# A decoder layer on one core: the second load of attention branch weights is issued ahead of the reads that spread the softmax reciprocals, and its pieces are split behind the rounding of the heads

## The chip, the core and the metric

The kernel runs on one core of a Trainium2 chip. The core has TensorE for matmuls (PE in the profile, with the weight load before each matmul as PEld), VectorE (DVE), ScalarE (ACT), GpSimd (POOL) and SyncE (SP). SP issues nearly all the transfers of this kernel; they go through one queue that 16 DMA engines serve. The metric is the device time of one execution in microseconds (us), the median of several runs; less is better.

## What is computed

One decoder layer on 256 tokens of width 1024, in float32, with random weights:

```python
h = rmsnorm(x, norm_mix_g)
proj = h @ w_in
q, k, v, u_pool, gate_logits = jnp.split(proj, [...], axis=-1)
q = apply_partial_rotary(rmsnorm(heads(q), q_norm_g), pos)      # 8 heads of 64
k = apply_partial_rotary(rmsnorm(heads(k), k_norm_g), pos)
attn = moba_attention(q, k, heads(v))    # 256 tokens are one block: causal softmax attention
pooled = multiscale_pool_mixer(u_pool, w_pool, pool_scale)
gates = jax.nn.sigmoid(gate_logits + b_gate).reshape(B, S, N_BRANCHES, D)
mixed = gates[:, :, 0] * (attn @ w_branch_attn) + gates[:, :, 1] * (pooled @ w_branch_pool)
x = x + mixed @ w_out
h2 = rmsnorm(x, norm_ffn_g)
up = causal_depthwise_conv(h2 @ w_up, conv_w, conv_b)
gate, val = jnp.split(up, 2, axis=-1)
return x + (jax.nn.silu(gate) * val) @ w_down
```

## The kernel before

**Matmuls in three.** A float32 product is made of three matmuls on rounded operands: each operand is split into a rounded high part (`hi`, written by ScalarE, `high`, L92) and the rest (`lo`, written by VectorE, `low`, L96), and `mm3` (L104 to L106) multiplies high by high, rest by high and high by rest. Every weight is therefore loaded raw, then split by ScalarE and VectorE, and only then used by TensorE.

**Weights as a list.** `order` lists all weight chunks of 1 MB in the order of use: q, k, v, pooling input (p), gates (g), pooling map, the pooling branch (`bp`, two chunks), the attention branch (`ba`, two chunks), the output projection (`o`, four) and the FFN. Four raw buffers exist (`RAWBUFS`), so chunk c can be loaded once chunk c-4 has been split. `load` issues the next one on SP, `loads` issues as many as have a free buffer. Each chunk is split in two pieces of 128 x 1024. `next_high` puts the high part of the next piece on ScalarE, unless its chunk is four or more ahead of the oldest one in use; `next_low` puts the rest on VectorE, one piece behind the high part, or at once with `eager=True`. `ahead()` does one of each.

**Engines run in program order.** Each engine works its instructions in the order in which they are written, so an instruction that waits holds up all behind it on that engine; the order is written out by hand. `later(n, fn)` puts a step off until `tick()` has been called n more times; `tick()` runs once for each of the 16 gate tiles and then at every odd j of the loop that follows.

**Attention to branches.** The softmax numerators (weights) of the last two head pairs are turned by VectorE, spilled to memory (`spill`), and read back transposed by `fill_weights` (SP, eight reads into `sm`). The sums' reciprocals go the same way: `turn_weights` spills them (`home_sums`, L297), and `fill_late` (L615) reads them back, spread over 64 partitions at a time, as `RS` (L623, two reads of 256 KB). `fill_late` also lets a weight load go ahead of these reads, and then takes off the brake on loads (`paused`).

**The loop of the pooling branch** (L738 to L753) runs over j = 0 to 7. Step j makes one tile `ps_bp` on TensorE (12 matmuls) in one of four PSUM banks, so step j needs the bank that step j-4 has given back. VectorE gives a bank back by multiplying the tile into its gate (L751, at j = 4 and 5 L741), and applies the norm's factor to one plain gate (L753). At j = 4 (`VALUES`) TensorE also makes `ps_o`, the attention values (L635, 32 matmuls), and `rounded` multiplies them by `RS` on VectorE (L654, four) and writes the high part of `heads` on ScalarE (four). At j = 5 `rests` writes the rest of `heads` on VectorE (four). In between, each j calls `ahead()` once.

**The loop of the attention branch** comes behind it: eight tiles `ps_ba` (L104 to L106) from `heads` and the `ba` chunks, in the same four banks. VectorE multiplies each into its gate (L766), GpSimd adds the other branch (L767), ScalarE and VectorE write `mh` and `ml`, and the output projection `ps_out` reads these.

Of the kernel before, what the change touches and what calls it, by code (L numbers as in the profile page):

```python
# [55 lines left out]
MAPS = 6  # L56
VALUES = 4
LATE = 9
GATES = (4, 5, 0, 1, 2, 6, 7, 3)
PLAIN = (4, 5, 6, 7, 8, 9)  # L60
HALVED = 2
# [10 lines left out]
def hybrid_layer_kernel(ctx: ExitStack, tc: tile.TileContext, xq_d, xtok_d, par_d, wkv_d, wpg_d,  # L72
# [21 lines left out]
    def low(lo, hi, src, scale=None):  # L94
        if scale is None:
            nc.vector.tensor_tensor(lo, src, hi.bitcast(F32), ALU.subtract)  # L96
        else:
            nc.vector.scalar_tensor_tensor(lo, src, scale, hi.bitcast(F32), ALU.mult, ALU.subtract)
# [11 lines left out]
    order += [("v", wkv_d[2 + c]) for c in range(2)] + [("p", wpg_d[c]) for c in range(2)]  # L110
    order += [("g", wpg_d[2 + c]) for c in GATES[:MAPS]] + [("pool", wpool_d)]
    order += [("g", wpg_d[2 + c]) for c in GATES[MAPS:]]
    order += [("bp", wbp_d[c]) for c in range(2)] + [("ba", wba_d[c]) for c in range(2)]
# [10 lines left out]
    def load(parts=1):  # L124
        c = loaded[0]
        if c == len(order):
            return
        loaded[0] += 1
        name, src = order[c]
        n = src.shape[-1]  # L130
        if c in cut_loads:
            parts = 2
        raws[c] = raw_p.tile([P, CH], F32, tag="raw", name=f"raw_{name}{c}")
        for i in range(parts):
            sl = slice(i * n // parts, (i + 1) * n // parts)
            nc.sync.dma_start(out=raws[c][:, sl], in_=src[:, sl])

    def raw(c, sl):

        if order[c][0] != "q":  # L140
            return raws[c][:, sl]
        at = sl.start % 512
        return xq[:, 4 * c + sl.start // 512, S + at:S + at + sl.stop - sl.start]
# [21 lines left out]
    def next_high():  # L165
        if at[0] < len(pieces):
            c, sl, first, _ = pieces[at[0]]
            if c - oldest() >= WBUFS:
                return
            at[0] += 1  # L170
            if first:
                moving = order[c][0] in "qkv"
                place = MOVING if moving else 0
                his[c] = whi_p.tile([P, CH + P], F32R, tag="whi", name=f"hi_{order[c][0]}{c}")[:, place:]
                place = MOVING if moving else FAR
                los[c] = wlo_p.tile([P, CH + P], F32R, tag="wlo", name=f"lo_{order[c][0]}{c}")[:, place:]
            high(his[c][:, sl], raw(c, sl))

    def next_low(eager=False):
        if at[1] < at[0] - STAGGER or at[0] == len(pieces) > at[1] or (at[1] < at[0] and eager):  # L180
            c, sl, _, last = pieces[at[1]]
            at[1] += 1
            low(los[c][:, sl], his[c][:, sl], raw(c, sl))
            if last:
                split.add(c)
                loads()
# [3 lines left out]
    def loads(most=None):  # L190

        while loaded[0] - RAWBUFS in split and order[loaded[0] - RAWBUFS][0] != "q" and loaded[0] < len(order):
            if paused[0] if most is None else most == 0:
                break
            load()
            most = most if most is None else most - 1
# [3 lines left out]
    def ahead(upto=0):  # L200

        next_high()
        next_low()
        if at[1] - sum(p[0] < used[0] for p in pieces) < upto:
            next_high()
            next_low()

    def chunk(name):
        c = used[0]
        used[0] += 1  # L210
        spent.update(i for i in range(c) if order[i][0] != "dn")
        assert order[c][0] == name and all(p[0] != c or name == "dn" and p[3] for p in pieces[at[1]:]), (name, order[c][0])
        return his[c], los[c]
# [130 lines left out]
    def big(name):  # L344
        return tmp.tile([P, 2 * 2 * 3 * P], F32, tag="big", bufs=2, name=name)
# [87 lines left out]
    def later(n, fn, *args):  # L433
        due.setdefault(clock[0] + n, []).append((fn, args))

    def tick():
        clock[0] += 1
        for fn, args in due.pop(clock[0], []):
            fn(*args)
# [80 lines left out]
    def gate(n):  # L520
        return gates[:, n // 2, n % 2, :]
# [27 lines left out]
    def scores():  # L549
        for hp in (0, 2, 3, 1):  # L550
            pss[hp] = score_steps(hp)

    def masked(hps):
        if hps[0] == 0:
            ys, sms = big("y0"), big("sm0")
        else:
            sms, ys = (act.tile([P, 2 * 2 * 3 * P], F32, tag=tag, name=f"{name}2")
                       for tag, name in (("qk", "sm"), ("at", "y")))
        for i, hp in enumerate(hps):
            ps = pss[hp]  # L560
            on = slice(i * 6 * P, (i + 1) * 6 * P)
            sm = sms[:, on].rearrange("p (j c) -> p j c", j=2)
            mx = tmp.tile([P, 2, 2], F32, tag="mx", name=f"mx{hp}")
            for j in range(2):
                nc.vector.tensor_tensor(sm[:, j, TOK[0]], ps[j][:, 3 * P:4 * P], mask[:, 1, :], ALU.add)
            for j in range(2):
                for t in (1, 0):
                    nc.vector.tensor_tensor_reduce(sm[:, j, TOK[t]], ps[j][:, TOK[t]],
                                                   whole if t else sm[:, j, TOK[0]], 1.0, LOWEST,
                                                   ALU.add, ALU.max, mx[:, t, j:j + 1])  # L570
            nc.vector.scalar_tensor_tensor(mx, mx, -1.0, qs[:, :, 2 * hp:2 * hp + 2], ALU.mult, ALU.mult)
            if i == 0:
                exponentials(hp, sm, mx, ys[:, on], sms[:, on])
            else:
                behind.append((exponentials, hp, sm, mx, ys[:, on], sms[:, on]))
# [35 lines left out]
    def fill_weights(hp, home, sm):  # L611
        fill(home, sm)
        soft[hp] = sm.rearrange("p (a n r) -> p a n r", a=4, r=32)

    def fill_late(far):  # L615

        for weights in late:
            fill_weights(*weights)
        loads(1)
        RS.append(big("RS"))  # L620
        for j in range(2):
            src = far.rearrange("(a i) r -> a (i r)", a=4)[None, :, j * S:(j + 1) * S].to_broadcast([DH, 4, S])
            nc.sync.dma_start(out=RS[0][j * DH:(j + 1) * DH, 0:H // 2 * S].rearrange("p (a c) -> p a c", a=4), in_=src)  # L623
        paused[0] = False
        loads()
# [22 lines left out]
    def rounded(hps, po):  # L648
        if not heads:
            both = act.tile([P, 2, KA, S], F32R, tag="at", name="heads")  # L650
            heads.extend(both[:, i] for i in range(2))
        for i, hp in enumerate(hps):
            v = weighed(hp)
            nc.vector.tensor_tensor(v, po[:, i, 0:S].rearrange("p (a t r) -> p a t r", a=4, r=32), v, ALU.mult)  # L654
            high(tokens(heads[0], hp), natural(hp))
# [31 lines left out]
    for n in range(2 * KD):  # L687
# [7 lines left out]
        if n == 6:  # L695
            scores()
        if n in (6, LATE):
            masked((0, 1) if n == 6 else (2, 3))
        if n == LATE - 1:
            paused[0] = True  # L700
# [12 lines left out]
        held.clear()  # L713
        f = 2 * GATES[b] + c
        if n in PLAIN:
# [10 lines left out]
    def branch(src, oph, opl, j, w):  # L726
        hi, lo = w
        ps = bank(f"ps_b{src}{j}")
        for k in range(4):
            sl = slice(k * 512 + (j % 4) * P, k * 512 + (j % 4 + 1) * P)  # L730
            mm3(ps[:, 0:S], (hi[:, sl], lo[:, sl]), (oph[:, k, :], opl[:, k, :]), k == 0, k == 3)
        return ps

    for j in range(KD):
        if j % 4 == 0:
            w = chunk("bp")
        ps = branch("p", poolh, pooll, j, w)
        if j == VALUES:  # L738
            pos = [(hps, values(hps)) for hps in ((0, 1), (2, 3))]
        if j in (VALUES, VALUES + 1):  # L740
            nc.vector.tensor_tensor(gate(KD + j), ps[:, 0:S], gate(KD + j), ALU.mult)  # L741
            for hps, po in pos:
                rounded(hps, po) if j == VALUES else rests(hps)
        if j % 2 == 1:
            tick()
            ahead()
        if j in (0, 2, 4, 6):
            ahead()
        sigmoids(1)
        if j not in (VALUES, VALUES + 1):  # L750
            nc.vector.tensor_tensor(gate(KD + j), ps[:, 0:S], gate(KD + j), ALU.mult)  # L751
        if j < len(plain):
            nc.vector.tensor_tensor(gate(plain[j]), gate(plain[j]), R1, ALU.mult)  # L753
# [264 lines left out]
```

## Time and profile before

| what | us |
|---|---|
| median of 3 runs | 333.08 (331.98 to 333.25) |
| the profiled execution, its own time | 332.71 |
| its span in the profile | 330.9 |
| TensorE matmul busy | 324.2 |
| VectorE busy | 259.3 |
| ScalarE busy | 202.0 |
| GpSimd busy | 71.4 |

How to read it: the span runs from the first to the last instruction, and the profiled execution's own time is 1.8 us longer. A matmul is pipelined: its row says 276 ns, but the next one starts 0.11 us after it, so TensorE is "busy" without a break as long as matmuls follow each other. Rows of a timeline give start, duration, engine, line, operation, output and inputs; "[0.53 <-DVE xq L751]" at a row's end says that the engine was idle for 0.53 us before it and that VectorE's instruction on L751 ended that. Names that end in q (SPq) are an engine's sequencer, here the issue of a transfer; the landing of a transfer is in the view of DMA issues.

### The profile page before, as it was taken

The page shows a single profiled execution, that of the slowest core. Times are in us where ns is not written, and L with a number is a line of the kernel's source. Part 1 is how long each engine was busy: PE and PEld are TensorE (multiplying, and loading weights), DVE is VectorE, ACT ScalarE, POOL GpSimd, SP SyncE. Part 2 cuts the span into 40 slices and gives each one's busy share as a digit, 9 for nine tenths or more (in the row PEclk, how much of TensorE's full clock was granted, in tenths as well). Part 3 has the DMA queues.
Part 4 walks back from the last instruction along what each step waited for, and adds up shares of the span by engine and source line. Part 5 has one row for each costly group of instructions (what it writes and reads, how often), then busy time and mean ns, then how long its engine had stood idle before and what let it go on. Part 6 is the DMA issues. An engine that isn't in the chain of part 4 may idle for free.

```text
span 330.9 us, 6770 instructions
## 1 busy us (share of the span) xinstructions
PE 324.2 (98%) x2708; PEld 316.8 (96%) x2708; DVE 259.3 (78%) x451; ACT 202.0 (61%) x329; POOL 71.4 (22%) x89
## 2 busy tenths in 40 slices
PE   8999999999999799999999999999999999999996
PEld 8888899999998699999999999999999999999995
DVE  4939989989974976878997977777777776768844
ACT  5767618566955756768676766564646464646520
POOL 1007690000000043130331212121212121221330
PEclk9999999999999999999999999999999999999999
DMA  7999799737699741763629274545455555553003
GB/s 265 425 415 215 241 367 292 277 131 280 229 267 361 261 186 18 254 240 128 210 64 360 104 282 146 237 150 236 169 213 165 218 184 198 193 189 129 0 2 127
DMA packets 16542, 69.72 MB, mean 211 GB/s; under 512 B 2176, under 2 KB 7040, under 8 KB 9856
## 3 DMA queue, kind: packets, MB, share of 16 engines
q1 hardware_dynamic: 16096, 69.17, 59.6%
q8 instruction: 21, 0.34, 0.4%
q10 hardware_dynamic: 416, 0.13, 0.3%
q14 instruction: 9, 0.07, 0.1%
HBM read 65.61 MB, written 3.69 MB: 209 GB/s over the span
## 4 chain that ended last, share of the span: by engine, by line
PE 80%; DVE 10%; DMA 5%; POOL 1%; issue 1%; ACT 1%; SPq 0%; DVEq 0%; POOLq 0%
PE ps_up L105 12%; PE ps_up L104 12%; PE ps_up L106 12%; PE ps_d L879 6%; PE ps_d L878 6%; PE ps_d L880 6%; PE ps_q L334 4%; DMA raw_o<-in_wout 3%; PE ps_k L334 3%; PE ps_v L334 3%; PE ps_out L105 2%; PE ps_out L106 2%; PE ps_out L104 2%; DMA raw_bp<-in_wbp 2%; PE ps_g L104 2%; PE ps_g L106 2%
## 5 line engine op out<-in xcount | busy, mean ns | idle before, releaser
L106 PE MATMUL ps_up<-hhi,lo_up 128*128 128x256 f32 x352 | 97.2, 276 | 0.0
L104 PE MATMUL ps_up<-hhi,hi_up 128*128 128x256 f32 x352 | 97.2, 276 | 0.0
L105 PE MATMUL ps_up<-hlo,hi_up 128*128 128x256 f32 x352 | 97.2, 276 | 0.0
L105 PEld LDWEIGHTS ps_up<-hlo,hi_up 128*128 128x128 f32 x352 | 66.1, 188 | 0.0
L104 PEld LDWEIGHTS ps_up<-hhi,hi_up 128*128 128x128 f32 x352 | 66.1, 188 | 0.0
L106 PEld LDWEIGHTS ps_up<-hhi,lo_up 128*128 128x128 f32 x352 | 66.1, 188 | 0.0
L96 DVE TENSOR_TENSOR lo_up<-raw_up,hi_up 128x1024 fp32r<-128x1024 f32 x44 | 54.7, 1261 | 7.3 <-ACT hi_up L92 7.3
L880 PE MATMUL ps_d<-ah,lo_dn 128*128 128x256 f32 x176 | 48.6, 276 | 0.0
L878 PE MATMUL ps_d<-ah,hi_dn 128*128 128x256 f32 x176 | 48.6, 276 | 0.0
L879 PE MATMUL ps_d<-al,hi_dn 128*128 128x256 f32 x176 | 48.6, 276 | 0.0
L92 ACT ACTIVATE hi_up<-raw_up 128x1024 fp32r<-128x1024 f32 x44 | 44.1, 1046 | 0.0
L860 POOL TENSOR_TENSOR c_v<-c_g,c_v 128x256 f32<-128x256 f32 x22 | 16.2, 738 | 121.4 <-DVE c_v L843 121.4
L92 ACT ACTIVATE ah<-c_v 128x256 fp32r<-128x256 f32 x22 | 9.2, 418 | 45.6 <-POOL c_v L860 45.6
L104 PE MATMUL ps_g<-xhi,hi_g 128*128 128x256 f32 x128 | 35.4, 277 | 0.0
L106 PE MATMUL ps_g<-xhi,lo_g 128*128 128x256 f32 x128 | 35.3, 276 | 0.0
L105 PE MATMUL ps_g<-xlo,hi_g 128*128 128x256 f32 x128 | 35.3, 276 | 0.0
L879 PEld LDWEIGHTS ps_d<-al,hi_dn 128*128 128x128 f32 x176 | 33.0, 188 | 0.0
L878 PEld LDWEIGHTS ps_d<-ah,hi_dn 128*128 128x128 f32 x176 | 33.0, 188 | 0.0
L880 PEld LDWEIGHTS ps_d<-ah,lo_dn 128*128 128x128 f32 x176 | 33.0, 188 | 0.0
L96 DVE TENSOR_TENSOR lo_dn<-raw_dn,hi_dn 128x1024 fp32r<-128x1024 f32 x22 | 27.8, 1264 | 0.4 <-ACT hi_dn L92 0.4
L848 DVE TENSOR_TENSOR u_v<-ps_up,R 128x256 f32<-128x256 f32 x22 | 9.3, 421 | 20.9 <-PE ps_up L106 20.8
L885 POOL TENSOR_TENSOR al<-c_v,ah 128x256 fp32r<-128x256 f32 x22 | 22.0, 1002 | 11.6 <-ACT ah L92 11.6
(189 smaller groups left out, 781.5 us busy)
## 6 DMA issues: line engine op xcount, KB each, us to landing
raw_up<-in_wup SPq DMA_DIRECT2D x22, 1024.0 KB, 4.8
raw_g<-in_wpg SPq DMA_DIRECT2D x8, 1024.0 KB, 7.4
raw_dn<-in_wdn SPq DMA_DIRECT2D x8, 1024.0 KB, 4.9
raw_o<-in_wout SPq DMA_DIRECT2D x4, 1024.0 KB, 11.1
raw_dn<-in_wdn SPq DMA_DIRECT2D x6, 512.0 KB, 4.9
raw_v<-in_wkv SPq DMA_DIRECT2D x2, 1024.0 KB, 15.5
raw_p<-in_wpg SPq DMA_DIRECT2D x2, 1024.0 KB, 13.0
raw_bp<-in_wbp SPq DMA_DIRECT2D x2, 1024.0 KB, 5.6
```

The costliest lines, as they stand in the source:

```text
L92: nc.scalar.activation(hi, src, AF.Copy, scale=scale)
L96: nc.vector.tensor_tensor(lo, src, hi.bitcast(F32), ALU.subtract)
L104: nc.tensor.matmul(out, sh, mh, start=start, stop=False, **kw)
L105: nc.tensor.matmul(out, sh, ml, start=False, stop=False, **kw)
L106: nc.tensor.matmul(out, sl, mh, start=False, stop=stop, **kw)
L334: nc.tensor.matmul(pt[t][:, c:c + wide], sx[:, k, t * P:(t + 1) * P], wx[:, sl], start=k == 0 and c == 0 and sx is xhi and wx is hi, stop= ...
L848: nc.vector.tensor_tensor(u, ps[:, 0:S], R2, ALU.mult)
L860: nc.gpsimd.tensor_tensor(uc[1], g[1], uc[1], ALU.mult)
L878: nc.tensor.matmul(o, hi[:, sl], acch[i], start=first, stop=False, skip_group_check=True)
L879: nc.tensor.matmul(o, hi[:, sl], accl[i], start=False, stop=False, skip_group_check=True)
L880: nc.tensor.matmul(o, lo[:, sl], acch[i], start=False, stop=i == KF - 1, skip_group_check=True)
L885: nc.gpsimd.tensor_tensor(accl[i], act_i, acch[i].bitcast(F32), ALU.subtract)
```

## The change

```diff
+PIECES = (1, 1, 0, 0, 0, 2, 1, 1)
 ...
 def fill_late(far):
     for weights in late:
         fill_weights(*weights)
+    loads(1)
+    later(1, spread, far)
+
+def spread(far):
+
     loads(1)
     RS.append(big("RS"))
     for j in range(2):
 ...
         if j % 2 == 1:
             tick()
+        for _ in range(PIECES[j]):
             ahead()
-        if j in (0, 2, 4, 6):
-            ahead()
+        if j == 2:
+            next_low(eager=True)
         sigmoids(1)
```

`fill_late` issues one weight load (ba0, the first chunk of the attention branch) and puts the reads of `RS` off by a tick into `spread`, which issues one more load (ba1, the second chunk) ahead of them. In the loop of the pooling branch, `ahead()` is no longer called once for each j, but 1, 1, 0, 0, 0, 2, 1 and 1 times; at j = 2 the rest of the third piece is written at once. The lines behind the change stand 1 to 7 lower in the new file (L751 is L758, L654 is L660).

On SP the place is the end of the reads of the attention weights (`sm`). Before:

```order
L305 DMA sm_1007<-home_w_1102 32x4x192 x4
L136 DMA raw_ba_1145<-in_wba 128x2048
L623 DMA RS<-home_sums 64x4x256 x2
L136 DMA raw_ba_1170<-in_wba 128x2048
L136 DMA raw_o_1237<-in_wout 128x2048
```

Now:

```order
L306 DMA sm_1007<-home_w_1102 32x4x192 x4
L137 DMA raw_ba_1145<-in_wba 128x2048
L137 DMA raw_ba_1192<-in_wba 128x2048
L629 DMA RS<-home_sums 64x4x256 x2
L137 DMA raw_o_1237<-in_wout 128x2048
```

The second load of `ba` has changed places with the two reads of `RS`; nothing else moved on SP.

On VectorE the place is j = 4 to 7 of the loop of the pooling branch, from the multiplication by `RS` on; `lo_ba` is the rest of the last piece of ba1, `lo_o` that of the first piece of the output weights, and xq holds the gates. Before:

```order
L654 TENSOR_TENSOR RS<-ps_o_1393,RS 128x4x64 x2
L654 TENSOR_TENSOR RS<-ps_o_1402,RS 128x4x64 x2
L96 TENSOR_TENSOR lo_ba_1338<-raw_ba_1170,hi_ba_1337 128x1024
L753 TENSOR_TENSOR xq<-xq,R_169 128x256
L741 TENSOR_TENSOR xq<-ps_bp_1429,xq 128x256
L96 TENSOR_TENSOR heads<-RS,heads 128x256 x4
L96 TENSOR_TENSOR lo_o_1422<-raw_o_1237,hi_o_1421 128x1024
L753 TENSOR_TENSOR xq<-xq,R_169 128x256
L751 TENSOR_TENSOR xq<-ps_bp_1451,xq 128x256
```

Now:

```order
L660 TENSOR_TENSOR RS<-ps_o_1392,RS 128x4x64 x2
L660 TENSOR_TENSOR RS<-ps_o_1401,RS 128x4x64 x2
L760 TENSOR_TENSOR xq<-xq,R_169 128x256
L747 TENSOR_TENSOR xq<-ps_bp_1422,xq 128x256
L97 TENSOR_TENSOR heads<-RS,heads 128x256 x4
L97 TENSOR_TENSOR lo_ba_1338<-raw_ba_1192,hi_ba_1337 128x1024
L760 TENSOR_TENSOR xq<-xq,R_169 128x256
L97 TENSOR_TENSOR lo_o_1442<-raw_o_1237,hi_o_1441 128x1024
L758 TENSOR_TENSOR xq<-ps_bp_1449,xq 128x256
```

The rest of ba1's last piece went from ahead of the rests of `heads` to behind them, and `lo_o` went behind the next multiplication of a gate (L753).

On ScalarE the place is the same stretch, from the high part of ba1's first piece on; xq<-xq,par are the sigmoids of the gates. Before:

```order
L92 ACTIVATE hi_ba_1337<-raw_ba_1170 128x1024
L666 ACTIVATE xq<-xq,par 128x256
L92 ACTIVATE hi_ba_1337<-raw_ba_1170 128x1024
L666 ACTIVATE xq<-xq,par 128x256 x2
L92 ACTIVATE heads<-RS 128x256 x4
L92 ACTIVATE hi_o_1421<-raw_o_1237 128x1024
```

Now:

```order
L93 ACTIVATE hi_ba_1337<-raw_ba_1192 128x1024
L672 ACTIVATE xq<-xq,par 128x256 x3
L93 ACTIVATE heads<-RS 128x256 x4
L672 ACTIVATE xq<-xq,par 128x256
L93 ACTIVATE hi_ba_1337<-raw_ba_1192 128x1024
L93 ACTIVATE hi_o_1441<-raw_o_1237 128x1024
```

The high part of ba1's last piece went from ahead of the high parts of `heads` to behind them. TensorE's and GpSimd's rows are the same as before.

## The prediction

> **What bounds the kernel now.** The page first. TensorE is busy for nearly the whole span and heads the chain that ended last; only VectorE and transfers take a visible share of that chain besides.
>
> ```profile
> PE 324.2 (98%) x2708; PEld 316.8 (96%) x2708; DVE 259.3 (78%) x451; ACT 202.0 (61%) x329; POOL 71.4 (22%) x89
> PE 80%; DVE 10%; DMA 5%; POOL 1%; issue 1%; ACT 1%; SPq 0%; DVEq 0%; POOLq 0%
> ```
>
> So a change can gain only where TensorE waits. The view of waits, for PE alone, names these waits, and but for the start there are two, both in the stretch that the change touches:
>
> ```profile
> PE ps_ba L105 <- DVE heads L96: 1.7, 1, 1.7
> PE ps_bp L104 <- DVE xq L751: 0.5, 1, 0.5
> ```
>
> TensorE's timeline shows their places, and a third place where single matmuls stand apart:
>
> ```profile
> 106.15 0.82 PE L635 MATMUL ps_o<-sm,vn 128*64 128x256 f32 x8
> ...
> 108.27 0.28 PE L106 MATMUL ps_bp<-poolh,lo_bp 128*128 128x256 f32 x1
> 109.07 0.39 PE L104 MATMUL ps_bp<-poolh,hi_bp 128*128 128x256 f32 x1 [0.53 <-DVE xq L751]
> ...
> 111.91 0.28 PE L104 MATMUL ps_ba<-heads,hi_ba 128*128 128x256 f32 x1
> 113.86 0.38 PE L105 MATMUL ps_ba<-heads,hi_ba 128*128 128x256 f32 x1 [1.67 <-DVE heads L96]
> ...
> 126.53 0.28 PE L106 MATMUL ps_out<-mh,lo_o 128*128 128x256 f32 x1
> 126.72 0.38 PE L104 MATMUL ps_out<-mh,hi_o 128*128 128x256 f32 x1
> 127.25 0.39 PE L105 MATMUL ps_out<-ml,hi_o 128*128 128x256 f32 x1
> 127.47 0.28 PE L106 MATMUL ps_out<-mh,lo_o 128*128 128x256 f32 x1
> ```
>
> Without a wait the next matmul starts 0.11 us after the last. By that pace j = 6 (109.07) starts 0.69 late, the second matmul of `ps_ba` (113.86) 1.84 late, each with one slow restart (0.11 more), and the output projection loses 0.08, 0.42 and 0.11 at 126.72, 127.25 and 127.47. Together some 3.4 us: about what there is to win.
>
> What ends these waits is VectorE, and what held VectorE is seen on its own timeline and ScalarE's:
>
> ```profile
> 99.30 1.06 ACT L92 ACTIVATE hi_ba<-raw_ba 128x1024 fp32r<-128x1024 f32 x1 [1.05 <-DMA raw_ba<-in_wba]
> 102.41 0.50 ACT L666 ACTIVATE xq<-xq,par 128x256 f32<-128x256 f32 x1
> 106.36 1.06 ACT L92 ACTIVATE hi_ba<-raw_ba 128x1024 fp32r<-128x1024 f32 x1 [3.46 <-DMA raw_ba<-in_wba]
> ```
>
> ```profile
> 101.53 0.41 DVE L751 TENSOR_TENSOR xq<-ps_bp,xq 128x256 f32<-128x256 f32 x1
> 104.01 0.41 DVE L753 TENSOR_TENSOR xq<-xq,R 128x256 f32<-128x256 f32 x1
> 107.45 1.22 DVE L96 TENSOR_TENSOR lo_ba<-raw_ba,hi_ba 128x1024 fp32r<-128x1024 f32 x1 [3.03 <-ACT hi_ba L92]
> 108.60 0.42 DVE L751 TENSOR_TENSOR xq<-ps_bp,xq 128x256 f32<-128x256 f32 x1
> ...
> 110.27 1.40 DVE L654 TENSOR_TENSOR RS<-ps_o,RS 128x256 f32<-128x256 f32 x4
> 111.59 1.21 DVE L96 TENSOR_TENSOR lo_ba<-raw_ba,hi_ba 128x1024 fp32r<-128x1024 f32 x1
> ...
> 113.39 1.42 DVE L96 TENSOR_TENSOR heads<-RS,heads 128x256 fp32r<-128x256 f32 x4
> ...
> 116.87 0.41 DVE L766 TENSOR_TENSOR xq<-ps_ba,xq 128x256 f32<-128x256 f32 x1
> ```
>
> ScalarE waited 3.46 us for ba1 to land, VectorE 3.03 for ScalarE. From 107.45 to 116.87, 9.42 us, no VectorE row has a bracket: it works off a backlog. Bank 2 comes back late (L751 at 108.60, TensorE's first wait), the rests of `heads` come late (the second), and the first tile of the attention branch is taken only at 116.87. **The bound is the landing of ba1.** It is set by its place in the queue. The issues and landings, from SP's timeline and the view of DMA issues over windows that hold one issue each (last figure: us to landing):
>
> ```profile
> 93.95 0.43 SPq L136 DMA_DIRECT2D raw_ba<-in_wba  x1
> raw_ba<-in_wba SPq DMA_DIRECT2D x1, 1024.0 KB, 5.2
> 94.43 0.68 SPq L623 DMA_DIRECT2D RS<-home_sums  x1
> 95.15 0.66 SPq L623 DMA_DIRECT2D RS<-home_sums  x1
> RS<-home_sums SPq DMA_DIRECT2D x1, 256.0 KB, 7.4
> 95.90 0.56 SPq L136 DMA_DIRECT2D raw_ba<-in_wba  x1
> raw_ba<-in_wba SPq DMA_DIRECT2D x1, 1024.0 KB, 10.4
> 96.57 0.36 SPq L136 DMA_DIRECT2D raw_o<-in_wout  x1
> raw_o<-in_wout SPq DMA_DIRECT2D x1, 1024.0 KB, 12.2
> 97.42 0.33 SPq L136 DMA_DIRECT2D raw_o<-in_wout  x1
> raw_o<-in_wout SPq DMA_DIRECT2D x1, 1024.0 KB, 13.8
> ```
>
> They land in order of issue: ba0 at 93.95 + 5.2 = 99.15, the second read of `RS` at 102.55, ba1 at 106.3, the first two output chunks at 108.8 and 111.2. A megabyte with nothing small ahead of it follows 2.4 to 2.5 us behind the last; ba1 needed 7.15 behind ba0, so the reads of `RS`, half a megabyte, delayed it by 4.7.
>
> **The change, part by part.** It adds and removes no instruction; four moves are to be priced.
>
> *ba1 ahead of `RS`.* It takes the issue slot at 94.43, and lands one megabyte behind ba0, at 99.15 + 2.45 = 101.6. ScalarE's queue reaches its first piece behind the sigmoid of 102.41, which takes 0.40 with one more behind it, so at 102.81; the high part is ready at 103.87. VectorE is free at 104.01 + 0.34 = 104.35. So `lo_ba`, at 107.45 before, starts at 104.35: **3.10 us earlier**, with 1.6 us of slack for the landing (the high part must be ready by 104.35). Bank 2 is back at about 105.9, and TensorE asks for it at 108.39: the first wait goes whole.
>
> *`RS` behind ba1.* The same bytes in another order are through at 106.3, so `RS` lands by then (at 105.0, if its reads take the 3.4 us that they took behind ba0). VectorE wants it 2.82 us after `lo_ba` (107.45 to 110.27), at 107.17; the values are ready at 106.15 + 0.82 = 106.97. Cost nothing; cover 0.9 us, and each us beyond that costs one.
>
> *The last piece of ba1 behind the heads' rounding.* On VectorE 1.13 us leave the path to the rests of `heads`: these start at 107.17 + 4 x 0.33 + 0.33 (L753) + 0.33 (L741) = 109.16, where L741 finds its tile done at 108.27 + 0.28. TensorE reaches the second matmul of `ps_ba` 24 matmuls and one behind 108.39, at 111.2, and the rests are written at 0.33 us each from 109.6 on: the second wait goes whole, 1.6 us to spare. The piece itself is then run at 110.5 and needed only by the attention branch's fifth tile. Its high part stands on ScalarE behind the rounding (done at about 109.0) and a sigmoid, and is ready at 110.4, just in time. What is queued behind: L753, `lo_o`, and L751 for j = 6, which gives TensorE the bank of its third `ps_ba` tile. By the same durations that ends at 113.5; TensorE asks for it at 111.1 + 24 x 0.113 = 113.8. If this cover of 0.3 goes, the wait costs what is missing, at most a few tenths, as the three instructions were queued there before too.
>
> *The eager rest at j = 2 and the other pieces.* They keep `lo_ba` of the third piece where it was. Price: nothing.
>
> *How it reaches the end.* VectorE's work up to L766 is the same set in another order and was without idle, so L766 comes at 104.35 + 9.42 = 113.77, again 3.10 earlier. From there to 127.25 the chain of waits runs through VectorE, GpSimd and ScalarE, and moves as a whole:
>
> ```profile
> 116.94 0.34 DVE xq L766
> ...
> 126.70 0.50 DVE ml L96
> ...
> 127.25 0.39 PE ps_out L105
> ```
>
> TensorE alone would be there 3.3 us earlier (0.69 + 0.11 + 1.84 + 0.11 + 0.08 + 0.42), the chain 3.10; the later counts: **3.10**. Behind that no wait of PE is left in the view, and TensorE's work is the same, so the gain stays. The bounds of the sum: 3.3 at the best (VectorE could start 0.2 earlier before the values stop it), and, as the chain follows ba1's landing one to one from 103.3 on, about 1.1 if ba1 lands at 105.0, by the rate of the first rival below, and the 0.3 of cover at the third `ps_ba` tile is lost besides.
>
> The row for 98 to 101 us shows what the reads of `RS` did to the queue, beside one with whole megabytes; the last two columns are the busy share of the DMA engines and GB/s:
>
> ```profile
> 98.00:101.00 3.00, 3.00 (x28) 3.00 (x28) 0.61 (x1) 1.95 (x4) 0.00 (x0) 1.00 0.88 208
> 104.00:107.00 3.00, 3.00 (x35) 2.13 (x34) 0.43 (x2) 0.64 (x1) 0.00 (x0) 1.00 0.99 407
> ```
>
> The engines were as busy but moved half as much. At 407 GB/s half a megabyte (0.52 MB) would take 1.3 us, not 4.7. This is a rival below. The Trainium skill, "DMA: Bandwidth & Descriptors", section "Specifications", speaks for that rival: it gives line rate for transfers from 512 B on and a fabric ceiling of 435 GB/s, by which the reads of `RS`, in runs of 1 KB, would cost an estimated 1.2 us and the change would gain about 1.2 to 1.4. The rate of 208 GB/s and the 4.7 us of this trace speak against it.
>
> **The rivals.** *The reads of `RS` cost only their bytes* (1.3 us), and ba1 was late for another reason, such as its own slow landing. Then ba1 lands at 106.3 - 1.3 = 105.0, `lo_ba` starts 1.09 later at 106.1, and the gain is 1.35: about 331.5. For it: nothing shows the queue's order byte by byte. Against: the rates above.
>
> *ba0 shares the engines with ba1*, both landing near 101.6. Then `lo_ba` for ba0, and L751 behind it (101.53 before), come 2.4 later, at 103.9, and TensorE waits for that bank at j = 4 from 102.70; ScalarE reaches ba1 at 105.2, VectorE at 106.3, gain 1.15: 331.8. Against it: whole megabytes landed one by one.
>
> *The change doesn't do what it says*: ba1 lands near 106 whatever its place, as the engines are full till 111. The gain is then only the last piece's move; the backlog stays as long, and the end moves by 0 to 0.3: 333.
>
> *`RS` becomes the wait.* The large loads behind it (two output chunks, issued within 1.5 us) pass or starve the small reads. From a landing at 107.2 each us takes one from the gain; at 110.3 the gain is gone, since VectorE multiplied by `RS` at 110.27 before, and beyond that the kernel is slower. If `RS` lands only with the third output chunk, near 113.7, it is 3.4 slower: 336.5. For it: these reads have a larger share of the queue's time than of its bytes. Against it: before, they had a megabyte ahead and two behind and landed in their turn.
>
> **How the numbers follow.** The sum stands on the profiled execution: 332.71 - 3.10 = 329.6. The median of the runs shown is 0.37 higher, which gives 330.0; I take 329.8. Chances: the forecast 0.71, the cheap reads 0.12, the shared landing 0.07, no effect 0.06, `RS` late 0.04. About 0.5%, 1.7 us, is what a measurement of this kernel can tell from no change; that bound lies at 331.4. The forecast is below it but for its worst corner, the cheap reads and the shared landing lie about on it and mostly above: faster 0.76, within 0.20, slower 0.04. The range runs from the lowest run less the best gain, 331.98 - 3.3 = 328.7, to the median less the lower bound of the gain, 333.08 - 1.1 = 332.0; no effect and a late `RS` are left out.
>
> **What would show it.** Right: ba1 lands near 101.6; ScalarE's 3.46 us wait is gone; `lo_ba` starts near 104.4; TensorE has no row with a bracket at j = 6 or at `ps_ba`; `RS` lands between 105 and 106.3, and the last piece runs near 110.5. Wrong: a wait of L654 for `RS`, a new bracket at j = 4 (ba0 late) or at the third `ps_ba` tile (bank 2 late), or gaps of the output projection that grew by what the two waits lost.

## The result and the profile after

The changed kernel took 330.09 us, the median of nine runs (329.14 to 331.59); the kernel before took 332.08 (331.69 to 333.25, nine runs, the three shown ahead of the prediction among them; their median, 333.08, was 1.0 us higher). The ratio is 0.9933, with a 95% interval of 0.9911 to 0.9954: about 2.2 us faster, between 1.5 and 3.0. The profiled execution has a span of 328.6 us against 330.9.

The page's first lines read as before; TensorE still heads everything:

```profile
PE 323.1 (98%) x2708; PEld 315.7 (96%) x2708; DVE 259.8 (79%) x451; ACT 202.1 (62%) x329; POOL 71.9 (22%) x89
PE 81%; DVE 9%; DMA 6%; POOL 1%; issue 1%; ACT 1%; SPq 0%; DVEq 0%; POOLq 0%
```

The view of waits for PE has lost both old waits, and shows two new ones:

```profile
PE ps_bp L105 <- DVE xq L758: 0.8, 1, 0.8
PE ps_ba L105 <- DVE xq L758: 0.2, 1, 0.2
```

On TensorE's timeline the first stands at j = 4 of the pooling branch's loop and the second at the third tile of the attention branch. The last of these rows is the matmul of the output projection that stands below them as it was in the profile of before: it starts 2.40 us earlier.

```profile
102.74 0.35 PE L105 MATMUL ps_bp<-poolh,hi_bp 128*128 128x256 f32 x1 [0.79 <-DVE xq L758]
...
114.27 0.38 PE L105 MATMUL ps_ba<-heads,hi_ba 128*128 128x256 f32 x1 [0.16 <-DVE xq L758]
...
125.51 0.39 PE L106 MATMUL ps_out<-ml,hi_o 128*128 128x256 f32 x1
```

```profile
127.91 0.38 PE L105 MATMUL ps_out<-ml,hi_o 128*128 128x256 f32 x1
```

ScalarE's timeline (the first piece of ba0, the first of ba1) and VectorE's (the rest of ba1's first piece, `RS`, the rests of `heads`, the last piece, the first tile of the attention branch):

```profile
99.93 1.06 ACT L93 ACTIVATE hi_ba<-raw_ba 128x1024 fp32r<-128x1024 f32 x1 [0.83 <-DMA raw_ba<-in_wba]
...
103.96 1.06 ACT L93 ACTIVATE hi_ba<-raw_ba 128x1024 fp32r<-128x1024 f32 x1 [0.42 <-DMA raw_ba<-in_wba]
```

```profile
105.05 1.23 DVE L97 TENSOR_TENSOR lo_ba<-raw_ba,hi_ba 128x1024 fp32r<-128x1024 f32 x1
...
107.86 1.41 DVE L660 TENSOR_TENSOR RS<-ps_o,RS 128x256 f32<-128x256 f32 x4
...
109.85 1.42 DVE L97 TENSOR_TENSOR heads<-RS,heads 128x256 fp32r<-128x256 f32 x4
111.19 1.22 DVE L97 TENSOR_TENSOR lo_ba<-raw_ba,hi_ba 128x1024 fp32r<-128x1024 f32 x1
...
114.47 0.41 DVE L773 TENSOR_TENSOR xq<-ps_ba,xq 128x256 f32<-128x256 f32 x1
```

ScalarE's wait for ba1 fell from 3.46 to 0.42 us. VectorE's backlog begins at 105.05 instead of 107.45, and the first tile of the attention branch comes 9.42 us later, as before to the hundredth. So the difference of the two profiles (2.3 us of span) is the 2.40 us by which the backlog starts earlier. It was forecast to be 3.10.

At 105.05 the row has no bracket any more. Two things end there almost together: the high part of ba1's first piece is ready at 103.96 + 1.06 = 105.02, and VectorE itself is free only at 104.98 (the row before it starts at 104.65, and the next in line starts 0.33 later). VectorE's own time hangs on ba0, which was split from 99.93 on here and from 99.30 on in the profile of before.

### The profile page after: what moved, and what is told of

Same layout as the page of the kernel before. It is cut to its first block, busy times and chain, and to the rows that moved or that the text cites. A ratio compares the mean times of both kernels' runs of the same rounds, so it can differ in the third digit from the quotient of the medians.

```text
span 328.6 us, 6769 instructions
## 1 busy us (share of the span) xinstructions
PE 323.1 (98%) x2708; PEld 315.7 (96%) x2708; DVE 259.8 (79%) x451; ACT 202.1 (62%) x329; POOL 71.9 (22%) x89
## 4 chain that ended last, share of the span: by engine, by line
PE 81%; DVE 9%; DMA 6%; POOL 1%; issue 1%; ACT 1%; SPq 0%; DVEq 0%; POOLq 0%
PE ps_up L107 12%; PE ps_up L105 12%; PE ps_up L106 12%; PE ps_d L887 6%; PE ps_d L885 6%; PE ps_d L886 6%; DMA raw_o<-in_wout 4%; PE ps_q L335 3%; PE ps_k L335 3%; PE ps_v L335 3%; DMA raw_bp<-in_wbp 2%; PE ps_out L106 2%; PE ps_out L107 2%; PE ps_out L105 2%; PE ps_g L105 2%; PE ps_g L107 2%
```

## The experiments

Two theories had to be told apart, and two questions of size were open. **Q**: the end follows the start of VectorE's backlog, which ba1's landing sets; what is moved within the backlog does not matter. **P**: the gain comes from taking the last piece of ba1 off the path to the rests of `heads`. The questions: why ba1 landed 4 us behind ba0 and not 2.45, and what the reads of `RS` cost.

The table gathers every profile. "ba0" and "ba1" are the starts on ScalarE of the first high part of each chunk (the landing, where ScalarE waited for it), "backlog" the start on VectorE of the rest of ba1's first piece, "RS" that of the multiplication by `RS`, "tile" that of the first tile of the attention branch (L766 of before), "tile - backlog" the difference of the two, "rest" the span less "tile". All in us. In both_first ScalarE waited for neither chunk, in ba0_first not for ba0; the difference there is no distance of landings.

| kernel | ba0 | ba1 | ba1 - ba0 | backlog | RS | tile | tile - backlog | span | rest |
|---|---|---|---|---|---|---|---|---|---|
| before | 99.30 | 106.36 | 7.06 | 107.45 | 110.27 | 116.87 | 9.42 | 330.9 | 214.0 |
| before_again | 100.32 | 105.77 | 5.45 | 106.86 | 109.67 | 116.27 | 9.41 | 330.4 | 214.1 |
| pieces_only | 99.61 | 105.16 | 5.55 | 106.25 | 109.06 | 115.65 | 9.40 | 329.8 | 214.2 |
| half_rs | 99.95 | 105.05 | 5.10 | 106.14 | 108.94 | 115.54 | 9.40 | 329.6 | 214.1 |
| the change | 99.93 | 103.96 | 4.03 | 105.05 | 107.86 | 114.47 | 9.42 | 328.6 | 214.1 |
| again | 99.69 | 103.85 | 4.16 | 104.94 | 107.75 | 114.35 | 9.41 | 328.5 | 214.2 |
| load_only | 99.34 | 103.59 | 4.25 | 104.68 | 107.48 | 114.09 | 9.41 | 328.2 | 214.1 |
| rs_behind | 99.35 | 103.16 | 3.81 | 104.41 | 109.00 | 115.61 | 11.20 | 329.7 | 214.1 |
| ba0_first | 96.53 | 102.92 | 6.39 | 104.01 | 106.82 | 113.42 | 9.41 | 327.5 | 214.1 |
| both_first | 97.36 | 100.86 | 3.50 | 102.39 | 106.25 | 113.72 | 11.33 | 327.8 | 214.1 |

Whatever was changed, the last column stays within 0.2 us: once the first tile of the attention branch is taken, the time to the end is the same.

### load_only: the loads without the pieces

```diff
-        for _ in range(PIECES[j]):
+            ahead()
+        if j in (0, 2, 4, 6):
             ahead()
-        if j == 2:
-            next_low(eager=True)
```

> Only the loads change places (ba1 ahead of the reads of RS); the pieces stay where they were. Theory Q (the end moves with the start of VectorE's backlog, which ba1's landing sets): VectorE's work up to the first tile of the attention branch (L766 of before) is the same set, so nearly the whole gain of the change stays: 2.0 us or a little less, ratio 0.993 to 0.995; TensorE waits for the rests of heads by 0.3 to 1 us, and the output projection's gaps shrink in turn. Theory P (the gain comes from taking the last piece off the path to the heads): little is left, ratio 0.997 to 1.000.

The diff is against the change. Measured: 329.59 us, ratio 0.9909 (0.9884 to 0.9934): the whole gain is there, and a little more of it than theory Q was expected to give (0.993 to 0.995). VectorE's timeline of this kernel, with the last piece of ba1 back ahead of the rests of `heads`:

```profile
104.68 1.23 DVE L96 TENSOR_TENSOR lo_ba<-raw_ba,hi_ba 128x1024 fp32r<-128x1024 f32 x1 [0.20 <-ACT hi_ba L92]
...
108.81 1.22 DVE L96 TENSOR_TENSOR lo_ba<-raw_ba,hi_ba 128x1024 fp32r<-128x1024 f32 x1
...
110.61 1.42 DVE L96 TENSOR_TENSOR heads<-RS,heads 128x256 fp32r<-128x256 f32 x4
...
114.09 0.42 DVE L771 TENSOR_TENSOR xq<-ps_ba,xq 128x256 f32<-128x256 f32 x1
```

The expected wait of TensorE for the rests of `heads` did not come: they start at 110.61, and that is early enough. The backlog is again 9.41 long. Q stands.

### pieces_only: the pieces without the loads

```diff
         for weights in late:
             fill_weights(*weights)
         loads(1)
-        later(1, spread, far)
-    def spread(far):
-        loads(1)
         RS.append(big("RS"))
```

> Only the pieces move; ba1 stays behind the reads of RS. Theory Q: VectorE's backlog starts near 107.4 us as before and L766 stays near 116.9, ratio 0.998 to 1.001; TensorE's second wait (for the rests of heads) shrinks by about 1.1 us, and the output projection gives that back. Theory P: most of the gain, ratio 0.993 to 0.996.

Again the diff is against the change. Measured: 332.36 us, ratio 0.9996 (0.9978 to 1.0013). P falls. (The backlog starts at 106.25 and not near 107.4, as expected from the one profile of before; before_again, below, shows that its 107.45 was late.) The view of waits for PE shows what became of the second wait:

```profile
PE ps_ba L105 <- DVE xq L753: 1.0, 1, 1.0
PE ps_ba L106 <- DVE heads L97: 0.3, 1, 0.3
```

The wait for `heads` fell to 0.3 us, and a wait of 1.0 for a PSUM bank has appeared at the third tile of the attention branch, 4 us later: the bank comes back late, since VectorE works off the same set. A wait was moved, not removed.

### again and before_again: a second look at each

> The changed kernel once more, for a second profile of it. If the 0.6 us by which ba0 landed later than in the profile of before was chance, ba0 lands at another time here, and the start of the rest of ba1's first piece follows it; ba1 lands about 4 us behind ba0 again if the reads behind it share the engines with it, 2.5 us if the 4 us were chance. Ratio 0.991 to 0.996 either way.

Measured: 330.08 us, ratio 0.9918 (0.9887 to 0.9949). ba0 was split at 99.69 and ba1 at 103.85, 4.16 behind it. The wait at j = 4 is gone here (its first matmul starts 0.12 us after the last), and the span is the same: that wait cost nothing.

> The kernel before once more, for a second profile of it. Theory Q: the span is the start of the rest of ba1's first piece plus 223.5 us (9.41 to the first tile of the attention branch, 214.1 from there) in this profile as in those so far. The distance from ba0's landing to ba1's was 7.15 us in the first profile and 5.55 where only the pieces were moved; if the first was chance, it is below 6.5 here, and the profile's span below 330.5.

Measured: one run of 332.18 us, span 330.4. ScalarE's and VectorE's rows:

```profile
100.32 1.06 ACT L92 ACTIVATE hi_ba<-raw_ba 128x1024 fp32r<-128x1024 f32 x1 [2.26 <-DMA raw_ba<-in_wba]
...
105.77 1.06 ACT L92 ACTIVATE hi_ba<-raw_ba 128x1024 fp32r<-128x1024 f32 x1 [1.84 <-DMA raw_ba<-in_wba]
```

```profile
106.86 1.23 DVE L96 TENSOR_TENSOR lo_ba<-raw_ba,hi_ba 128x1024 fp32r<-128x1024 f32 x1 [1.41 <-ACT hi_ba L92]
...
116.27 0.42 DVE L766 TENSOR_TENSOR xq<-ps_ba,xq 128x256 f32<-128x256 f32 x1
```

The distance of 7.06 us was indeed a long one: 5.45 here. The profile on which the prediction stood had a backlog that started later than usual. Over the three profiles with the old order of loads and both reads the backlog starts at (107.45 + 106.86 + 106.25) / 3 = 106.85, over the change, again and load_only at (105.05 + 104.94 + 104.68) / 3 = 104.89: 1.96 us, against 1.99 between the medians. Three profiles each, which differ by up to 1.2 us among themselves, can't show that so closely: the agreement to the hundredth is luck.

### half_rs: what the reads of RS cost

```diff
+        nc.gpsimd.memset(RS[0][DH:P, 0:H // 2 * S], 1.0)
-        for j in range(2):
+        for j in range(1):
             src = far.rearrange(...)
```

> The kernel before, with one of the two reads of RS left out (its half of RS is filled with ones by GpSimd), in the old order. Theory Q with costly reads: ba1 lands 4 to 5 us behind ba0 instead of 5.5 to 7.15, the rest of ba1's first piece starts 1.2 to 2.3 us earlier, ratio 0.993 to 0.997. Rival (the reads cost only their bytes, 0.65 us for one): ba1 lands 0.65 us earlier, ratio 0.998 or above.

Measured: 331.18 us, ratio 0.9969 (0.9952 to 0.9987), and ba1 5.10 us behind ba0. The distance is short of 5.45 and 5.55 by 0.4, and of the first profile's 7.06 by 2.0: it misses the expected 4 to 5, so one profile cannot price the reads. The ratio can: half of them cost about 0.31%, 1.0 us (0.4 to 1.6), so by doubling it an estimate of 2 us for both, the whole gain of the change. The table says the same in another way: ba1 came 7.06, 5.45 and 5.55 us behind ba0 with the reads ahead of it, and 4.03, 4.16 and 4.25 with the reads behind it, 1.9 us less on average. The prediction's 4.7 us for the reads is far too much. The price of bytes alone (0.65 us for one, 1.3 for both) isn't excluded by either.

### rs_behind: the reads of RS behind an output chunk

```diff
     def spread(far):
         loads(1)
+        paused[0] = False
+        loads()
+        later(2, reads, far)
+    def reads(far):
         RS.append(big("RS"))
         ...
-        paused[0] = False
-        loads()
```

> The change, with the reads of RS issued one place later still, behind the first output chunk, so that a whole megabyte and nothing small stands behind ba1. Theory S (small reads behind a load share the engines with it, which is why ba1 lands 4.1 to 4.25 us behind ba0 and not 2.45): ba1 lands 2.4 to 2.9 us behind ba0, and ScalarE does not wait for it. Rival (the second of two loads takes 4 us anyway): 4 us again. In both, RS lands later, at 107.5 to 109.5 us, VectorE waits at the multiplication by RS for up to 2 us, and the end follows that multiplication: ratio 0.992 to 0.999, not better than the change.

Measured: 332.08 us, ratio 1.0004 (0.9984 to 1.0025): the gain is gone, and the ratio lies above the expected 0.992 to 0.999. ba1 and then `RS`, on ScalarE and on VectorE:

```profile
103.16 1.06 ACT L93 ACTIVATE hi_ba<-raw_ba 128x1024 fp32r<-128x1024 f32 x1 [0.20 <-DMA raw_ba<-in_wba]
```

```profile
104.41 1.22 DVE L97 TENSOR_TENSOR lo_ba<-raw_ba,hi_ba 128x1024 fp32r<-128x1024 f32 x1
...
109.00 1.42 DVE L664 TENSOR_TENSOR RS<-ps_o,RS 128x256 f32<-128x256 f32 x4 [1.71 <-DMA RS<-home_sums]
...
115.61 0.42 DVE L777 TENSOR_TENSOR xq<-ps_ba,xq 128x256 f32<-128x256 f32 x1
```

VectorE begins its backlog at 104.41, here as soon as it is free itself, and waits 1.71 us for `RS`, and the tile is taken 6.61 behind that multiplication, as everywhere without a wait in between (before: 116.87 - 110.27 = 6.60). So the rival "`RS` becomes the wait" is real, and one megabyte too late in the queue is enough for it. With a whole megabyte behind it ba1 still lands 3.81 us behind ba0, not 2.4 to 2.9: theory S explains some 0.2 to 0.4 of it by this one profile, and falls as the main cause.

### ba0_first and both_first: can more be had?

Two further orders on SP: ba0 ahead of the eight reads of attention weights, and both chunks ahead of them.

```diff
     def fill_late(far):
+        loads(1)
         for weights in late:
             fill_weights(*weights)
-        loads(1)
         later(1, spread, far)
```

> The change, and ba0 too is issued earlier, ahead of the eight reads of attention weights instead of behind them. Theory Q with the bound now at ba0 (its issue waits until the pooling branch's second chunk has landed, and ScalarE then waits for ba0): ba0 lands before 98.5 us, ScalarE's wait for it goes, the wait of TensorE for the first bank goes, ba1 is then split up to 1 us earlier, and the kernel gains another 0.3 to 1 us, ratio 0.990 to 0.993. Rival: the reads of attention weights, now behind a megabyte more, land after 104 us and hold the values: ratio 0.995 or above, with a wait of TensorE at L635 of before.

Measured: 329.54 us, ratio 0.9925 (0.9899 to 0.9952), not distinguishable from the change. ba0 is no longer waited for, but ba1, behind the eight reads, is; SP's timeline, the view of DMA issues and ScalarE's timeline:

```profile
96.01 0.38 SPq L137 DMA_DIRECT2D raw_ba<-in_wba  x1
raw_ba<-in_wba SPq DMA_DIRECT2D x1, 1024.0 KB, 6.8
102.92 1.06 ACT L93 ACTIVATE hi_ba<-raw_ba 128x1024 fp32r<-128x1024 f32 x1 [2.80 <-DMA raw_ba<-in_wba]
```

```diff
     def fill_late(far):
-        for weights in late:
-            fill_weights(*weights)
-        loads(1)
         later(1, spread, far)
     def spread(far):
-        loads(1)
+        loads(2)
+        for weights in late:
+            fill_weights(*weights)
```

> The change, with both loads of attention branch weights ahead of the eight reads of attention weights. ba0 and ba1 land before 101 us, ScalarE waits for neither; the rest of ba1's first piece then starts at 103.5 or earlier, and the multiplication by RS at about 107.0, when the values are done, 0.5 to 0.9 us earlier than in the change: ratio to before 0.988 to 0.992. Rival: RS or the attention weights, now last in the queue, land after 107 or 104 us and hold VectorE or the values: ratio 0.994 or above, with a wait of VectorE at L654 of before or of TensorE at L635 of before.

Measured: 329.19 us (329.05 to 329.63), ratio 0.9911 (0.9893 to 0.9928). VectorE's timeline:

```profile
106.25 0.76 DVE L659 TENSOR_TENSOR RS<-ps_o,RS 128x256 f32<-128x256 f32 x2 [0.97 <-DMA RS<-home_sums]
107.21 0.76 DVE L659 TENSOR_TENSOR RS<-ps_o,RS 128x256 f32<-128x256 f32 x2 [0.20 <-PE ps_o L640]
...
108.77 0.42 DVE L746 TENSOR_TENSOR xq<-ps_bp,xq 128x256 f32<-128x256 f32 x1 [0.47 <-PE ps_bp L107]
...
113.72 0.42 DVE L772 TENSOR_TENSOR xq<-ps_ba,xq 128x256 f32<-128x256 f32 x1
```

Here no weight load bounds the stretch any more: VectorE waits 0.97 us for `RS`, now last in the queue, then 0.20 for TensorE's values and 0.47 for its tile of j = 5. So the wait that the rival named is there, but the ratio is not the rival's. TensorE has no wait there in its view. Its median is the lowest of all, but its interval covers that of the change; that it beats the change isn't shown, only that it beats the kernel before.

## Why the prediction was right, and where its size was off

- *The bound is the landing of ba1*: right for the kernel before. With ba1 earlier the two waits of TensorE went, and in every profile in which VectorE waited for nothing behind the backlog's start, the span is that start plus 9.4 plus 214.1.
- *The gain passes to the end undiminished*: right. 2.40 us at the backlog's start, 2.40 at the output projection, 2.3 in the span.
- *The reads of `RS` delayed ba1 by 4.7 us*: the mechanism was right, the size was not. By the distances of the table the delay is 1.9 us on average. The prediction had one profile, in which ba1 came 7.06 us behind ba0; the next two have 5.45 and 5.55.
- *ba1 lands at 99.15 + 2.45 = 101.6*: too early. The 2.45 was taken from loads deeper in the queue (ba1, then the two output chunks); the second of two loads issued back to back came 4.03 to 4.25 behind the first, and 3.81 with a megabyte behind it. That used up the 1.6 us of slack, but cost only 0.07 to 0.29 us more.
- *The backlog starts 3.10 earlier, at 104.35*: this is the term that was mis-sized; it started at 105.05, 104.94 and 104.68. VectorE itself was free at 104.98, 104.74 and 104.39 there, since ba0 was split from 99.93, 99.69 and 99.34 on and not from 99.30. So of the 0.54 us by which the mean of 104.89 lies behind 104.35, some 0.35 are ba0's and 0.19 are ba1's.
- *The 107.45 it was counted from* was one execution's, 0.6 later than the mean of three. Together: 3.10 - 0.6 - (104.89 - 104.35) = 1.96.
- *The time, 329.8*: 0.3 from the 330.09 measured, while the gain came out at 2.2 where 333.08 - 329.8 = 3.3 was forecast. That is not luck alone: the time rests on the backlog's start at 104.35, which was 0.54 off, while the gain also has in it the late landing of ba1 in the profile of before.
- *The last piece of ba1 off the path to the heads*: what it moves was right, and it was put at no gain of its own, as the set of VectorE's work stays the same. pieces_only and load_only show that: 0.9996 without the loads, 0.9909 with the loads alone.
- *`RS` lands by 106.3, cover 0.9 us*: it landed at about 106.6 (96.49 + 10.1), ahead of the multiplication at 107.86, with 1.3 us to spare. The cover held, and rs_behind shows what lies beyond it.
- *A new bracket at j = 4 would mean that ba0 is late*: it appeared, 0.79 us. It wasn't the shared landing of the second rival, as ba0 landed 5.0 us after its issue (5.2 before). The pooling branch's second chunk landed late in that execution (8.1 us from issue, 6.4 before), ba0 is issued only behind it, and VectorE gave the bank back 0.64 later (L758 at 102.17, L751 at 101.53 before); TensorE also came to it 0.9 earlier. In again and load_only the bracket is not there, and their spans are shorter than the change's only by what their backlogs start earlier (0.1 and 0.4 us).
- *A new bracket at the third `ps_ba` tile would mean that the cover of 0.3 is gone*: it appeared too, 0.16 us here and 0.30 in again. It cost nothing: in both, the tile and the end follow the backlog's start as in load_only, where it is not there.
- *The reads cost only their bytes*, the first rival: its gain of 1.35 is about as far below the 2.2 measured as 3.10 is above it; its time of 331.5 is 1.4 off. Its price for the reads, 1.3 us, is nearer to the 1.9 measured than the forecast's 4.7, and is not excluded. Its reason, that the reads move at the full rate, doesn't fit the rates: between 98 and 101 us, where the prediction read 208 GB/s, the change, again and load_only moved 421, 403 and 410, and between 101 and 104, where the reads now stand, 251, 228 and 229 (before: 393).
- *ba1 lands near 106 whatever its place*, the third rival, is ruled out by 103.96, 103.85 and 103.59.

Left open: why the second of two loads takes 3.8 us and more when later ones follow at 2.4 to 2.5. In rs_behind the engines moved 415 GB/s between the two starts of ScalarE (99.35 to 103.16), about 1.6 MB, half a megabyte more than ba1 holds: bytes of what stands behind ba1 moved before ba1 was complete. Which engine carried which is not shown.

## What to carry to other kernels

Where one engine works off a backlog without idle, as VectorE does here for 9.4 us, what starts the backlog sets the end, and reordering within it moves waits from one consumer to the next; look for the same distance between two rows in several profiles. Two things can start it, the data and the engine itself: once ba1 came earlier, VectorE's own time, and with it ba0, was within 0.3 us of it. A large load that a busy engine waits for belongs ahead of small reads that are needed later, as far as these have cover: 1.3 us of it were left here, and one more megabyte ahead of them took the gain back. Before a term is counted from one profile's landing, ask for a second profile: the distance of two landings differed by 1.6 us between two executions of one kernel.

## What the runs showed of the hardware

A load took longer to land with small reads behind it in the queue than with another load behind it. The pooling branch's second chunk, a megabyte, with eight reads of 96 KB right behind it took this long to land in before and in the change, and this long in ba0_first and both_first, where another megabyte stands right behind it (views of DMA issues, in this order). The 8.1 is the longest of eight profiles with the reads behind it, the other seven have 6.2 to 6.7:

```profile
raw_bp<-in_wbp SPq DMA_DIRECT2D x1, 1024.0 KB, 6.4
raw_bp<-in_wbp SPq DMA_DIRECT2D x1, 1024.0 KB, 8.1
raw_bp<-in_wbp SPq DMA_DIRECT2D x1, 1024.0 KB, 5.1
raw_bp<-in_wbp SPq DMA_DIRECT2D x1, 1024.0 KB, 5.4
```

And SP itself waits for that landing: the last of the eight reads is issued only when it is there (at 93.60, where the chunk landed at 87.23 + 6.4; in the change at 94.47 and 86.33 + 8.1), so that ba0 is issued behind it. Why that read waits for the chunk is not shown. The view of SP's waits, before and then the change:

```profile
SPq L305 <- DMA raw_bp<-in_wbp: 2.3, 1, 2.3
SPq L306 <- DMA raw_bp<-in_wbp: 4.0, 1, 4.0
```
